# A hybrid decoder layer on one core: right operands of the Strassen products made on GpSimd during retention, a later turning back of chunks, and a fifth pair of input tiles

## The chip, the cores and the metric

The kernel runs on one core of a Trainium2 chip. The metric is the device time of one execution in microseconds; the kernel before takes 1079.97 us (median of three runs, 1079.96 to 1080.04). In the profile PE is TensorE, DVE is VectorE, ACT is ScalarE, POOL is GpSimd and SP is SyncE, whose queue issues all DMAs here.

## What is computed

One decoder layer over 1024 positions with a model width of 1024, all in float32. Cut to what matters:

```python
u = rms_norm(x, norm1_g)
z = u @ w_in                      # 3*512 columns for conv, 4*512 for retention
y_conv = cb * causal_dwconv3(cc * ch, conv_w)          # then a group norm, 8 groups
q, k = rotary(rq), rotary(rk) * 128 ** -0.5
# retention, 4 heads, chunks of 128 positions
scores = (q_c @ k_c.T) * intra_decay
o = scores @ v_c + (q_c * xi) @ state
state = chunk_decay * state + (k_c * zeta).T @ v_c
y_ret = group_rms_norm(o, ret_norm_g, 4) * silu(rg)
x = x + concat(y_conv, y_ret) @ w_out
x = x + relu(rms_norm(x) @ w_up) ** 2 @ w_down
out = rms_norm(x, final_norm_g)
```

## The kernel before, in words

Everything is held transposed: features lie on the 128 partitions, positions along the row. A matmul takes a block of weights [128 x 128] and 512 positions. To keep float32 accuracy every operand is split into a rounded high half and the remainder, its low half, and each product is three matmuls (high-high, high-low, low-high). ACT casts the high half, DVE or POOL subtracts it for the low half (`split_piece`, L166, for weights).

SBUF has one large pool, `big` (L104), of 40 buffers of [128 x 1024], called units; all large tiles come from it and a new one waits until a buffer is free. Smaller tiles are `t` (pool `tp`, L111, six buffers), `h` for retention (six) and `s` for norms (four). The eight PSUM banks are two pools of four, `pm` and `pr`.

The program is written in the order of each engine's queue. A planner in Python decides at build time where background work goes: `Engine` (L48) keeps a clock for each engine by a linear cost, `now` is PE's time, `slot()` advances it by 2.72 us for twelve matmuls. Background tasks are generators; `tick()` (L501) after each twelve or so matmuls continues those whose engine would start within `LOOK` = 3.2 us. A generator yields what it waits for: a tuple of engines of which the one that ends first is taken, a key that another task marks, or a margin after which its matmuls may be put into PE's queue. `force(key)` (L461) runs all tasks until a key is marked.

The stages up to the output projection:

1. Load x, scale it by `norm1_g`, split it (uh, ul) and make v for all heads (L350, up to about 50 us). ACT copies v out of eight banks (L363).
2. Four rotary tile pairs: q and k for head pair p = 0, then p = 1 (`rot_tiles`, L540). Each tile is `tile_in` (L518): four quarters of 24 matmuls over two banks. DVE multiplies by cosine and sine out of the banks, DVE and POOL add.
3. `retention(p)` (L577), a background task, once q and k of its head pair are there. In one step chunk c gets its scores, and the transposed keys; DVE masks the scores and ACT scales the keys. One step later the chunk's product with v and the state is made, DVE updates the state S, and ACT and DVE norm the result (`m` holds two numbers for each position, `on` the normed chunk). One step after that PE turns the chunk back (L661) and ACT copies it out.
4. The remaining sixteen column tiles of w_in, in the order `IN_TURNS` (L40) and `IN_END`. Single tiles go by `whole` (L741), pairs by `pair_in` (L821). A pair uses a Strassen-like scheme of seven products for two tiles and two halves of positions (`UP_ORDER`, L45: 1, 2, 5, 6, 3, 7, 4), each of 12 matmuls over one bank. Its left operands are sums of weight blocks, made by POOL (`Left`, L198); its results are combined by DVE adds out of banks. Its right operands are the input halves "11", "21", "22", which are uh and ul themselves, and four sums t1 to t4 for each of four k tiles j. `rights(j)` (L782) makes these: it loads two xs tiles from HBM again, scales them on ACT (1024 columns at once), makes four sums on POOL or DVE, and for each sum a high half on ACT (`put_hi`) and a low half on POOL or DVE (`put_lo`) into a unit called U. Tiles j = 0, 1 start after retention of p = 0, j = 2, 3 after that of p = 1, and odd ones after the even one before. Before the first pair's products 5, 6, 7 and 4 the operand that they read is forced (L827).
5. Convolution, gates and norms run as background tasks on the outputs of these tiles. Then the last two tiles (`IN_END`) by halves, and the output projection from about 332 us.

The weight pieces follow in the same order as the tiles through SP's queue, four buffers in `rw`; `mix` is asked for a new piece whenever one is taken.

Of the kernel before, what the change touches and what calls it, by code (L numbers as in the profile page):

```python
# [16 lines left out]
P = 128  # L17
# [19 lines left out]


IN_QK = [12, 13, 16, 17, 14, 15, 18, 19]
IN_TURNS = [0, 1, 2, 3, 20, (4, 5), (6, 7), (8, 9), (10, 11), 21]  # L40
IN_END = [22, 23]
SLOT, LOOK, PE_MARGIN, LATE = 2.72, 3.2, 1.2, 0.0
WARM = 10
# [36 lines left out]
def hybrid_layer(  # L80
# [27 lines left out]
    banks_ = ctx.enter_context(ExitStack())  # L108
    pm = banks_.enter_context(tc.tile_pool(name="pm", bufs=4, space=PSUM))
    pr = banks_.enter_context(tc.tile_pool(name="pr", bufs=4, space=PSUM))  # L110
    tp = mixer.enter_context(tc.tile_pool(name="tp", bufs=6))  # L111
    xp = mixer.enter_context(tc.tile_pool(name="xp", bufs=1))

    ctx.enter_context(tc.manual_schedule())
# [226 lines left out]

    v = [unit(s="v") for _ in range(NC_ // 2)]
    rtok = cp.tile([P, NC_], F32, name="rtok")
    ms = xp.tile([P, NC_], F32, name="ms")
    r2 = xp.tile([P, NC_], F32, name="r2")
# [12 lines left out]
                        stop=(k == KT - 1 and a is ul),  # L360
                    )
    for c in range(NC_):
        act.copy(v[c // 2][:, hs[c % 2]], vb[c])  # L363

    def token_norms():
        b = bank(pr)
# [210 lines left out]
    def retention(p, q, k):  # L577

        h0 = 2 * p
        S = pend = turn = None  # L580
        o = q
        js = [slice(j * P, (j + 1) * P) for j in range(2)]
        if p:
            yield "retention", 0
        for c in range(NC_ + 2):
            yield STEP_MARGIN
            now[0] += 1.7
            new = None
            if c < NC_:
                sl = slice(c * P, (c + 1) * P)  # L590
                bs = bank(pr)
                for j in range(2):
                    nc.tensor.matmul(bs[:, js[j]], k[j][:, sl], q[j][:, sl], start=True, stop=True)
                kz = None
                if c < NC_ - 1:
                    bt = bs[:, 2 * P :]
                    for j in range(2):
                        nc.tensor.transpose(bt[:, js[j]], k[j][:, sl], ident)
                sc = xp.tile([P, 2 * P], F32, tag="h", name=nm("h"), bufs=6)
                for j in range(2):  # L600
                    dve.scalar_tensor_tensor(
                        sc[:, js[j]], bs[:, js[j]], by_key[:, h0 + j, c : c + 1], causal,
                        ALU.mult, ALU.mult,
                    )
                if c < NC_ - 1:
                    kz = xp.tile([P, 2 * P], F32, tag="h", name=nm("h"), bufs=6)
                    for j in range(2):
                        act.activation(
                            kz[:, js[j]], bt[:, js[j]], AF.Copy, scale=by_state[:, h0 + j, c : c + 1]
                        )  # L610
                new = (c, sc, kz)
                retention_task[p].ready = clock[dve]
            done, pend = pend, new
            turned, turn = turn, None
            if done is not None:
                pc, sc, kz = done
                psl = slice(pc * P, (pc + 1) * P)
                vt = v[pc // 2]
                v0 = (pc % 2) * H + h0 * P
                vj = [vt[:, v0 + j * P : v0 + (j + 1) * P] for j in range(2)]  # L620
                bo = bank(pr)
                for j in range(2):
                    nc.tensor.matmul(bo[:, js[j]], sc[:, js[j]], vj[j], start=True, stop=(S is None))
# [20 lines left out]
                on = xp.tile([P, 2 * P], F32, tag="h", name=nm("h"), bufs=6)  # L644
# [12 lines left out]
            if turned is not None:  # L657
                pc, on = turned
                b = bank(pr)
                for j in range(2):  # L660
                    nc.tensor.transpose(b[:, js[j]], on[:, js[j]], ident)  # L661
# [89 lines left out]

        tile_in(evac)

    for p in range(2):
# [10 lines left out]
    U = {}  # L765

    def put_hi(name, j, src):
# [5 lines left out]
        hi, lo = U[name][j]  # L773
        eng.tensor_sub(lo, src, f32(hi))

    def product(n, bank_):
        name = {1: "11", 2: "21", 3: "22", 4: "t4", 5: "t1", 6: "t2", 7: "t3"}[n]
        b = bank(bank_)
        mm(parts.pop(0), [b], lambda _, k: U[name][k], True, True)
        return b  # L780

    def rights(j):  # L782

        yield "retention", j // 2
        if j % 2:
            yield "t4", j - 1
        a, b = (unit(s="xs") for _ in range(2))
        lo_, hi_ = hs
        for k, t in ((j, a), (4 + j, b)):
            nc.sync.dma_start(t, xT[k * P : (k + 1) * P, :])  # L790
        rights_task[j].ready = now[0] + 5.0
        for k, t in ((j, a), (4 + j, b)):
            yield (act,)
            act.activation(t, t, AF.Copy, scale=sm[:, G1 + k : G1 + k + 1])
        eng = yield (pool, dve)
        eng.tensor_sub(a[:, lo_], a[:, hi_], a[:, lo_])
        eng = yield (pool, dve)
        eng.tensor_sub(a[:, hi_], b[:, hi_], a[:, hi_])
        eng = yield (pool, dve)
        eng.tensor_sub(b[:, hi_], b[:, hi_], a[:, lo_])  # L800
        eng = yield (pool, dve)
        eng.tensor_sub(b[:, lo_], b[:, lo_], b[:, hi_])
        for name, src in (("t1", a[:, lo_]), ("t2", b[:, hi_]), ("t3", a[:, hi_]), ("t4", b[:, lo_])):
            yield (act,)
            put_hi(name, j, src)
            eng = yield (pool, dve)
            put_lo(name, j, src, eng)
            mark((name, j), eng)

    rights_task = []  # L810
    for j in range(4):
        rights_task.append(Task(rights(j), now[0]))
        rights_task[j].go()
    spread_norms(rows_)
    for j in range(4):
        for c, name in ((0, "11"), (1, "21"), (2, "22")):
# [707 lines left out]
```

## Time and profile before

| | |
|---|---|
| median of three runs | 1079.97 us |
| the profiled execution, its own time | 1082.14 us |
| its span (first to last instruction) | 1080.3 us |
| mean granted TensorE clock | 0.995 |
| HBM read, written | 71.40 MB, 9.44 MB |
| PE's chain share | 80% of the chain that ended last |

The span is what the trace covers; the execution's own time has what lies around it. The page gives for each engine its busy time, its share of the span and its number of instructions. In a list of groups, a row has the line, the engine and the operation, the tile written and the tiles read, the shapes and how many; behind the first bar the busy time in us and the mean of one in ns, behind the second the idle time of the engine just ahead of them and what ended it. L74 is the line of the helper that records every operation of ACT, DVE and POOL, so their groups are told apart by tiles. In an order of time a row begins with its start and its duration in us, and an idle time ahead of it stands in square brackets. In the list of waits the numbers are the total in us, how often, and the longest.

### The profile page before, as it was taken

The numbers are of one execution on the slowest core, as the hardware profiler recorded it, in microseconds if no ns is written. First come the engines' busy times: TensorE is split into PE (matmuls) and PEld (weight loads), VectorE is DVE, ScalarE is ACT, GpSimd is POOL, SyncE is SP. The second block draws the span as 40 slices with busy tenths as digits, with TensorE's granted clock in tenths as the row PEclk, the third lists the DMA queues.
The fourth block names the chain that finished last, engine by engine and source line by source line (L and its number), as shares of the span: only waits on it lengthen the run. The fifth ranks groups of instructions, "written<-read, shape, count | busy, mean of one in ns | idle before, by whom it ended". The sixth has DMA issues, their size and how long they took to land.

```text
span 1080.3 us, 14040 instructions
## 1 busy us (share of the span) xinstructions
PE 1060.6 (98%) x4936; PEld 882.7 (82%) x4936; DVE 881.2 (82%) x1255; ACT 463.3 (43%) x916; POOL 540.3 (50%) x370
## 2 busy tenths in 40 slices
PE   9999999999999999999999999999999999999996
PEld 7888888887778888788788888888888888888886
DVE  8446546799997666699999989999899899899945
ACT  8211445763335544444343443443343434334453
POOL 6233323256752132559548258267286295384543
PEclk9999999999999999999999999999999999999998
DMA  7121121212223635050121211211301211210204
GB/s 273 62 59 48 31 79 69 100 58 77 69 59 117 224 114 169 2 194 30 58 69 39 79 39 49 89 25 54 93 25 50 88 30 43 85 30 12 77 1 157
DMA packets 40311, 81.75 MB, mean 76 GB/s; under 512 B 4528, under 2 KB 6704, under 8 KB 40240
## 3 DMA queue, kind: packets, MB, share of 16 engines
q1 hardware_dynamic: 40240, 80.85, 23.2%
q8 instruction: 39, 0.64, 0.2%
q14 instruction: 32, 0.26, 0.1%
HBM read 71.40 MB, written 9.44 MB: 75 GB/s over the span
## 4 chain that ended last, share of the span: by engine, by line
PE 80%; DVE 11%; issue 3%; POOL 3%; ACT 2%; DMA 1%; POOLq 0%; DVEq 0%; SPq 0%; ACTq 0%
PE b L401 50%; PE b L1274 23%; PE b L355 4%; DVE z L74 2%; DVE wl L74 2%; POOL r L74 1%; POOL z L74 1%; DVE t L74 1%; DVE x L74 1%; DVE xs L74 1%; DVE U L74 1%; DVE q L74 1%; ACT h L74 1%; PE b L337 1%; DVE m L74 1%
## 5 line engine op out<-in xcount | busy, mean ns | idle before, releaser
L401 PE MATMUL b<-U,wh 128*128 128x512 f32 x1024 | 315.9, 390 | 2.4 <-DVE x L74 1.2
L74 ACT CAST wh<-r 128x512 fp32r<-128x512 f32 x286 | 175.9, 620 | 321.2 <-PE b L401 134.7
L74 DVE TENSOR_TENSOR wl<-r,wh 128x512 fp32r<-128x512 f32 x251 | 233.3, 932 | 90.9 <-ACT wh L74 90.0
L74 POOL TENSOR_TENSOR r<-r,r 128x512 f32<-128x512 f32 x136 | 209.8, 1545 | 116.0 <-DVE wl L74 65.6
L1274 PE MATMUL b<-V,wh 128*128 128x512 f32 x784 | 242.0, 389 | 0.7 <-POOL V L74 0.4
L401 PEld LDWEIGHTS b<-U,wh 128*128 128x128 f32 x1024 | 191.8, 188 | 43.4 <-issue 2.8
L74 DVE TENSOR_TENSOR x<-x,b 128x512 f32<-128x512 f32 (+1 forms) x320 | 197.8, 663 | 24.4 <-PE b L401 19.3
L401 PE MATMUL b<-U,wl 128*128 128x512 f32 x512 | 199.4, 389 | 0.0
L1274 PEld LDWEIGHTS b<-V,wh 128*128 128x128 f32 x784 | 147.0, 188 | 32.3 <-POOL V L74 0.8
L74 POOL TENSOR_TENSOR t<-t,t 128x512 f32<-128x512 f32 x70 | 106.3, 1523 | 97.9 <-ACT t L74 51.9
L1274 PE MATMUL b<-V,wl 128*128 128x512 f32 x392 | 152.5, 389 | 0.0
L74 POOL TENSOR_TENSOR wl<-r,wh 128x512 fp32r<-128x512 f32 x35 | 49.1, 1408 | 159.2 <-ACT wh L74 151.9
L401 PEld LDWEIGHTS b<-U,wl 128*128 128x128 f32 x512 | 96.0, 188 | 20.7 <-POOL wl L74 0.4
L401 PE MATMUL b<-uh,wh 128*128 128x512 f32 x304 | 103.3, 399 | 2.3 <-DVE z L74 2.3
L401 PE MATMUL b<-uh,wl 128*128 128x512 f32 x304 | 100.8, 392 | 1.1 <-DVE wl L74 1.1
L401 PE MATMUL b<-ul,wh 128*128 128x512 f32 x304 | 101.0, 392 | 0.0
L1274 PEld LDWEIGHTS b<-V,wl 128*128 128x128 f32 x392 | 73.6, 188 | 15.2
L74 POOL TENSOR_TENSOR V<-t,V 128x512 fp32r<-128x512 f32 x35 | 49.6, 1417 | 67.2 <-ACT V L74 67.2
L74 DVE TENSOR_TENSOR t<-t,b 128x512 f32<-128x512 f32 x112 | 75.8, 677 | 1.7 <-POOL t L74 1.2
L74 ACT ACTIVATE t<-t 128x512 f32<-128x512 f32 x64 | 40.2, 631 | 81.9 <-DVE t L74 81.3
L74 DVE TENSOR_TENSOR V<-t,V 128x512 fp32r<-128x512 f32 x63 | 70.3, 1116 | 0.0
L401 PEld LDWEIGHTS b<-uh,wl 128*128 128x128 f32 x304 | 57.3, 189 | 13.9 <-DVE wl L74 1.5
(168 smaller groups left out, 1431.0 us busy)
## 6 DMA issues: line engine op xcount, KB each, us to landing
r<-w_up_t SPq DMA_DIRECT2D x64, 256.0 KB, 2.6
r<-w_down_t SPq DMA_DIRECT2D x56, 256.0 KB, 2.7
r<-w_in_t SPq DMA_DIRECT2D x48, 256.0 KB, 2.6
xt<-xT SPq DMA_DIRECT2D x16, 256.0 KB, 5.4
xs<-xT SPq DMA_DIRECT2D x8, 512.0 KB, 4.8
r<-w_out_t SPq DMA_DIRECT2D x16, 256.0 KB, 2.7
x<-xT SPq DMA_DIRECT2D x8, 512.0 KB, 7.4
k<-x SPq DMA_DIRECT2D x6, 512.0 KB, 3.2
```

The costliest lines, as they stand in the source:

```text
L74: return f(out, *args, **kw)
L337: nc.tensor.matmul(b[:, c * P : (c + 1) * P], d, ident, start=True, stop=True)
L355: nc.tensor.matmul(vb[i], a[k][:, i * P : (i + 1) * P], b[k // 2][:, vs], start=(k == 0 and a is uh and b is vh), stop=(k == KT - 1 and a ...
L401: nc.tensor.matmul(b, a[:, k, :], rhs(n, k)[r], start=(start and i == 0), stop=(stop and i == len(ops) - 1),)
L1274: nc.tensor.matmul(b, a, r, start=(i == 0), stop=(i == len(ops) - 1))
```

## The change

Four things change together:

- **Order.** `IN_TURNS` begins with tile 20 and then 0 and 1; tiles 2 and 3 become a pair, so five pairs and four single tiles stand where four pairs and six single tiles stood.
- **Right operands.** `rights(j)` is started after q and k of the first head pair. Tile j = 0 starts after these, 1 after t4 of tile 0, 2 after q and k of the second pair, 3 after t1 of tile 2. High and low halves of j = 1 wait for retention of p = 0, those of 2 for t4 of tile 1, those of 3 for retention of p = 1. While a retention task is alive the sums and low halves go to POOL alone, afterwards to POOL or DVE. The scaling is in halves of 512 columns, and all four high halves come ahead of the low halves.
- **Turning back.** The normed chunk is turned back two steps after its product instead of one. Retention has one more step, and `h` has eight buffers.
- **v.** It is stored by head pair and half of the chunks, so that the first pair's part is free when its retention ends. Each bank is copied half by ACT and half by DVE. `t` has five buffers.

```diff
-IN_TURNS = [0, 1, 2, 3, 20, (4, 5), (6, 7), (8, 9), (10, 11), 21]
+IN_TURNS = [20, 0, 1, (2, 3), (4, 5), (6, 7), (8, 9), (10, 11), 21]
...
-    tp = mixer.enter_context(tc.tile_pool(name="tp", bufs=6))
+    tp = mixer.enter_context(tc.tile_pool(name="tp", bufs=5))
...
-    v = [unit(s="v") for _ in range(NC_ // 2)]
+    v = {(p, i): unit(s="v") for p in range(2) for i in range(2)}
...
-        act.copy(v[c // 2][:, hs[c % 2]], vb[c])
+        for p, eng in ((0, act.copy), (1, dve.tensor_copy)):
+            to = slice(c % 4 * 2 * P, (c % 4 + 1) * 2 * P)
+            eng(v[p, c // 4][:, to], vb[c][:, p * 2 * P : (p + 1) * 2 * P])
...
-        S = pend = turn = None
+        S = pend = None
+        turns = []
...
-        for c in range(NC_ + 2):
+        for c in range(NC_ + 3):
...
-                sc = xp.tile([P, 2 * P], F32, tag="h", name=nm("h"), bufs=6)
+                sc = xp.tile([P, 2 * P], F32, tag="h", name=nm("h"), bufs=8)
...
-            turned, turn = turn, None
+            turned = turns.pop(0) if turns and (len(turns) > 1 or c > NC_) else None
...
-                turn = (pc, on)
+                turns.append((pc, on))
...
             if c == NC_:
+                k = None
+                for i in range(2):
+                    del v[p, i]
                 mark(("retention", p), act)
...
+    def beside():
+
+        return (pool,) if any(t in procs for t in retention_task) else (pool, dve)
+
+    def rights(j):
+
+        yield [("qk", 0), ("t4", 0), ("qk", 1), ("t1", 2)][j]
+        a, b = (unit(s="xs") for _ in range(2))
+        lo_, hi_ = hs
+        for k, t in ((j, a), (4 + j, b)):
+            nc.sync.dma_start(t, xT[k * P : (k + 1) * P, :])
+        rights_task[j].ready = now[0] + 5.0
+        for k, t in ((j, a), (4 + j, b)):
+            yield (act,)
+            act.activation(t[:, lo_], t[:, lo_], AF.Copy, scale=sm[:, G1 + k : G1 + k + 1])
+            yield (act,)
+            act.activation(t[:, hi_], t[:, hi_], AF.Copy, scale=sm[:, G1 + k : G1 + k + 1])
+        eng = yield beside()
+        eng.tensor_sub(a[:, lo_], a[:, hi_], a[:, lo_])
...
+        if j:
+            yield [("retention", 0), ("t4", 1), ("retention", 1)][j - 1]
+        parts_ = ("t1", a[:, lo_]), ("t2", b[:, hi_]), ("t3", a[:, hi_]), ("t4", b[:, lo_])
+        for name, src in parts_:
+            yield (act,)
+            put_hi(name, j, src)
+        for name, src in parts_:
+            eng = yield beside()
+            put_lo(name, j, src, eng)
+            mark((name, j), eng)
...
+        mark(("qk", p), dve)
+        if p == 0:
+            for j in range(4):
+                rights_task.append(Task(rights(j), now[0]))
+                rights_task[j].go()
...
-    def rights(j):
-
-        yield "retention", j // 2
-        if j % 2:
-            yield "t4", j - 1
...
-            act.activation(t, t, AF.Copy, scale=sm[:, G1 + k : G1 + k + 1])
-        eng = yield (pool, dve)
...
-            put_hi(name, j, src)
-            eng = yield (pool, dve)
-            put_lo(name, j, src, eng)
-            mark((name, j), eng)
```

More of the change, by code (lines that the diff above doesn't have):

```diff
@@ L605, in retention @@
                 if c < NC_ - 1:
-                    kz = xp.tile([P, 2 * P], F32, tag="h", name=nm("h"), bufs=6)
+                    kz = xp.tile([P, 2 * P], F32, tag="h", name=nm("h"), bufs=8)
                     for j in range(2):
@@ L617, in retention @@
                 psl = slice(pc * P, (pc + 1) * P)
-                vt = v[pc // 2]
-                v0 = (pc % 2) * H + h0 * P
+                vt = v[p, pc // 4]
+                v0 = pc % 4 * 2 * P
                 vj = [vt[:, v0 + j * P : v0 + (j + 1) * P] for j in range(2)]
@@ L642, in retention @@
                     retention_task[p].ready = clock[dve]
-                on = xp.tile([P, 2 * P], F32, tag="h", name=nm("h"), bufs=6)
+                on = xp.tile([P, 2 * P], F32, tag="h", name=nm("h"), bufs=8)
                 m = xp.tile([P, 2], F32, tag="m", name=nm("m"), bufs=4)
@@ L752, in whole, with put_hi, put_lo @@
         tile_in(evac)
+    U = {}
+    def put_hi(name, j, src):
+        u = unit(F32R, "U")
+        act.copy(u[:, :H], src)
+        U.setdefault(name, [None] * 4)[j] = (u[:, :H], u[:, H:])
+    def put_lo(name, j, src, eng=dve):
+        hi, lo = U[name][j]
+        eng.tensor_sub(lo, src, f32(hi))
+    def beside():
[15 more added lines that the diff above has]
+        eng = yield beside()
+        eng.tensor_sub(a[:, hi_], b[:, hi_], a[:, hi_])
+        eng = yield beside()
+        eng.tensor_sub(b[:, hi_], b[:, hi_], a[:, lo_])
+        eng = yield beside()
+        eng.tensor_sub(b[:, lo_], b[:, lo_], b[:, hi_])
+        if j:
[5 more added lines that the diff above has]
+        for name, src in parts_:
+            eng = yield beside()
+            put_lo(name, j, src, eng)
+            mark((name, j), eng)
+    rights_task = []
     for p in range(2):
@@ L762, in hybrid_layer @@
         del q, k
-    U = {}
-    def put_hi(name, j, src):
-        u = unit(F32R, "U")
-        act.copy(u[:, :H], src)
-        U.setdefault(name, [None] * 4)[j] = (u[:, :H], u[:, H:])
-    def put_lo(name, j, src, eng=dve):
-        hi, lo = U[name][j]
-        eng.tensor_sub(lo, src, f32(hi))
+        mark(("qk", p), dve)
[3 more added lines that the diff above has]
+                rights_task[j].go()
     def product(n, bank_):
@@ L780, in product @@
         return b
-    def rights(j):
-        yield "retention", j // 2
-        if j % 2:
-            yield "t4", j - 1
[L787 to L793, printed above, removed]
-            act.activation(t, t, AF.Copy, scale=sm[:, G1 + k : G1 + k + 1])
-        eng = yield (pool, dve)
-        eng.tensor_sub(a[:, lo_], a[:, hi_], a[:, lo_])
-        eng = yield (pool, dve)
[L798 to L804, printed above, removed]
-            put_hi(name, j, src)
-            eng = yield (pool, dve)
-            put_lo(name, j, src, eng)
-            mark((name, j), eng)
[L810 to L813, printed above, removed]
     spread_norms(rows_)
```

## The prediction

> **What bounds the kernel now.** I read the page first, then PE's waits, then busy times by stage, then each engine in order of time around the waits.
>
> ```profile
> span 1080.3 us, 14040 instructions
> PE 1060.6 (98%) x4936; PEld 882.7 (82%) x4936; DVE 881.2 (82%) x1255; ACT 463.3 (43%) x916; POOL 540.3 (50%) x370
> ```
>
> PE is busy for 98% of the span, so the time is its number of matmuls plus its few waits. In this execution 1082.14 us were counted around a span of 1080.3; the median of the three runs is 1079.97. I make the sum as a difference in the span and take it from the median.
>
> All edits lie between 47 and 320 us. The waits of PE there, from 104 to 335 us:
>
> ```profile
> PE b L401 <- DVE z L74: 2.3, 1, 2.3
> PE b L661 <- ACT h L74: 1.2, 3, 0.6
> PE b L401 <- DVE wl L74: 1.1, 1, 1.1
> PE b L481 <- ACT s L74: 1.0, 1, 1.0
> PE b L482 <- DVE s L74: 0.4, 2, 0.2
> PE b L482 <- DVE r L74: 0.3, 1, 0.3
> ```
>
> That is 6.3 us in all. 1.2 of it is retention's turning back (L661); 5.1 belongs to the stretch of the pairs. Busy time there (PE, PEld, DVE, ACT, POOL, then granted clock):
>
> ```profile
> 104.00:160.00 56.00, 55.43 (x325) 48.17 (x325) 30.57 (x82) 24.52 (x97) 15.12 (x12) 1.00 0.16 53
> 160.00:209.00 49.00, 48.37 (x287) 42.27 (x286) 33.01 (x83) 28.92 (x100) 15.53 (x12) 1.00 0.21 75
> 209.00:318.00 109.00, 104.47 (x452) 83.63 (x450) 103.28 (x112) 53.53 (x91) 66.85 (x43) 1.00 0.23 75
> 318.60:322.20 3.60, 3.60 (x9) 2.88 (x10) 2.74 (x4) 1.75 (x3) 0.87 (x1) 0.55 0.00 0
> ```
>
> The reader is to see two regimes. While retention runs (the first two rows) DVE is busy 55% and 67%, POOL 27% and 32%. From 209 us on DVE is at 95%, and PE's waits there nearly all end on DVE. The last row: after the wait of 2.3 us the clock is granted at 0.55 for 3.6 us, which loses another 1.6 us (3.6 x 0.45).
>
> **Part by part: the fifth pair.** Two single tiles (2 and 3) are 2 x 4 quarters of 24 matmuls, a pair is 7 products of 12 over one bank: 7 x 12 = 84 in place of 2 x 48 = 96. Twelve fewer. Their price, from PE's order of time inside a pair, where the products follow without a gap:
>
> ```profile
> 243.72 0.39 PE L401 MATMUL b<-uh,wh 128*128 128x512 f32 x1
> 246.44 0.62 PE L401 MATMUL b<-U,wh 128*128 128x512 f32 x2
> ```
>
> From the first matmul of one product to the first of the next are 2.72 us. So -2.7 us, certain as long as PE sets the end. (A matmul's row of 0.39 us overlaps the next; the distance counts.)
>
> What the pair adds elsewhere: seven vector adds from banks, three more weight splits (seven pieces for four), four POOL sums of blocks; two ACT copies of a go. Groups from 205 to 320 us, with those for the right operands that leave this stretch:
>
> ```profile
> L74 DVE TENSOR_TENSOR z<-z,b 128x512 f32<-128x512 f32 x25 | 17.0, 680 | 0.5
> L74 DVE TENSOR_TENSOR wl<-r,wh 128x512 fp32r<-128x512 f32 x17 | 19.7, 1157 | 1.7 <-ACT wh L74 1.6
> L74 DVE TENSOR_TENSOR U<-xs,U 128x512 fp32r<-128x512 f32 x10 | 11.1, 1130 | 0.2
> L74 DVE TENSOR_TENSOR xs<-xs,xs 128x512 f32<-128x512 f32 x4 | 4.6, 1146 | 0.3
> L74 DVE TENSOR_TENSOR xs<-xs 128x512 f32<-128x512 f32 x4 | 3.8, 960 | 0.1
> L74 POOL TENSOR_TENSOR r<-r,r 128x512 f32<-128x512 f32 x16 | 24.5, 1535 | 4.0 <-DMA r<-w_in_t 2.0 <-DVE wl L74 1.3
> ```
>
> Added to DVE: 7 x 0.68 + 3 x 1.16 = 8.2 us; to POOL 4 x 1.54 = 6.1. Removed from DVE: 11.1 + 4.6 + 3.8 = 19.5 us, less up to 4 x 1.13 = 4.5 for the low halves of the fourth k tile, which may still go to either engine. Net relief about 6.8 us. But the stretch gets 2.7 us shorter, and tile 1's work on a (before, partly ahead of 205) now falls behind it, an estimate of 2.5 us from two bank products and an R2 product. So DVE has 103.3 - 6.8 + 2.5 = 99 us of work in some 106: 93% in place of 95%. I therefore take the 5.1 us of waits and the 1.6 us of slow clock as unchanged, ends at all of it gone (-6.7) and, as one more pair brings its share of them, at +1.7 (6.7 over four pairs).
>
> **The right operands earlier.** 32 element-wise instructions (16 sums, 16 low halves), before mostly on DVE after retention's middle; 24 of them, k tiles 0 to 2, can now only go to POOL while retention is alive. Both engines' times for one (shortest, median, longest):
>
> ```profile
> L74 DVE TENSOR_TENSOR U<-xs,U x13: 679/693/1789, 177.1 to 243.2; 128x512 fp32r<-128x512 f32 x13
> L74 POOL TENSOR_TENSOR U<-xs,U x3: 1287/1299/1728, 177.7 to 235.2; 128x512 fp32r<-128x512 f32 x3
> L401 PE MATMUL b<-U,wh x128: 387/389/402, 238.3 to 315.5; 128*128 128x512 f32 x128
> ```
>
> 24 x 1.30 = 31 us (at 1.73, 41) come to POOL's 15.1 + 15.5 from 104 to 209 us: 62 to 72 of 105. It fits. Against this speaks the Trainium skill, GPSIMD Engine Reference, section 4.1 (Engine selection): ordinary two-input arithmetic belongs on VectorE, about 2x faster; the trace agrees (1.30 to 0.69), and by that rule the sum would lose 24 x 0.6 = 15 us if these instructions lay on the path.
>
> Are they in time? The last row says that U is first read at 238.3 us. In the new order only tiles 20, 0, 1, twelve quarters, stand ahead of the first pair instead of twenty, so it starts about eight quarters of 2.7 earlier. PE's order of time at retention's end:
>
> ```profile
> 205.64 0.38 PE L623 MATMUL b<-v,h 128*128 128x128 f32 x2
> 209.79 0.52 PE L661 MATMUL b<-ident,h 128*128 128x128 f32 x2
> ```
>
> Retention's last product is at 206 us, the twelfth quarter ends at 209.8, and the first pair's third product (the first with t1) comes two products later, at 215.2. Only the fourth k tile waits for that last product; then it needs a cast and a low half, about 2 us, for t1, and at most 4 x 1.73 = 7 us for all four, the last of which is read at about 226. So zero, hidden by two products on uh and ul; if POOL is behind by more than some 7 us, the excess comes straight onto PE.
>
> The xs loads go through SP's queue ahead of weight fetches; the weights are taken three pieces ahead, some 16 us, and a load waits only for a buffer to come free. Zero, up to +2. The scaling in two halves of 512 instead of one of 1024 adds only instruction starts on ACT, half idle in these rows.
>
> **The turn two steps later.** PE waited 1.2 us in three places for the normed chunk. The longest:
>
> ```profile
> 194.75 0.97 DVE L74 TENSOR_TENSOR m<-m 128x2 f32<-128x2 f32 x1 [0.27 <-ACT m L74]
> 195.76 1.19 DVE L74 SCALAR_TENSOR_TENSOR m<-m,m 128x2 f32<-128x2 f32 x1
> 193.17 1.29 POOL L74 TENSOR_TENSOR wl<-r,wh 128x512 fp32r<-128x512 f32 x1 [9.21 <-ACT wh L74]
> 194.43 1.27 POOL L74 TENSOR_TENSOR a<-a,ssq 128x512 f32<-128x512 f32 x1
> 195.67 1.25 POOL L74 TENSOR_TENSOR xs<-xs 128x512 f32<-128x512 f32 x1
> 197.86 0.44 PE L661 MATMUL b<-ident,h 128*128 128x128 f32 x2 [0.63 <-ACT h L74]
> ```
>
> A [128 x 2] instruction that takes 0.16 us alone (row below) takes 0.97 and 1.19 while POOL runs without a break. With a step more, about 5 us, this is covered: -1.2 us. No matmul is added, only the last transposes move; the two more h buffers keep a chunk alive and are paid by one t buffer. Evacuation needs four t at once and a norm one each, so five do: zero.
>
> **v in halves.** The eight copies of v are shared by ACT and DVE, behind PE's product and ahead of nothing before retention at 104: zero.
>
> Sum: -2.7 - 1.2 = -3.9, or 1079.97 - 3.9 = 1076.1; ends -3.9 - 6.7 = -10.6 (1069.4) and -3.9 + 1.7 + 2 = -0.2 (1079.8) without the rivals. I say 1076.0.
>
> **The rivals.** *The pairs' waits go* (0.20). With no backlog of right operands, DVE reaches the last pair's adds in time: the 2.3 us wait, its 1.6 us of slow clock, and half of the other 2.8 vanish: 1076.1 - 5.3, about 1071. For it: 18 DVE instructions leave; against:
>
> ```profile
> 247.84 2.46 DVE L74 SCALAR_TENSOR_TENSOR cv<-a,sm,cv 128x511 f32<-128x511 f32 x2 [0.85 <-ACT cv L74]
> ```
>
> DVE stood idle for 0.85 us at 247, so that backlog was over before the waits of the pairs. The Trainium skill, TensorE: Matmul & The Clock Gate, section "What's actually happening", gives an idle window of about 3.4 us before the clock is halved; here 2.3 us were enough.
>
> *The vector engine eats it* (0.16). The fifth pair's 8.2 us on DVE and 6.1 on POOL come in a stretch at 95%; half of DVE's share, 4 us, turns into new waits: 1080, no change.
>
> *Slower: POOL holds up retention* (0.14). DVE works in order: the next chunk's masking stands behind this chunk's m instructions. One step on DVE with POOL still:
>
> ```profile
> 117.94 0.61 DVE L74 SCALAR_TENSOR_TENSOR h<-b,bk,causal 128x128 f32<-128x128 f32 x2 [1.73 <-PE b L598]
> 121.34 0.16 DVE L74 SCALAR_TENSOR_TENSOR m<-m 128x2 f32<-128x2 f32 x1
> 122.93 0.61 DVE L74 SCALAR_TENSOR_TENSOR h<-b,bk,causal 128x128 f32<-128x128 f32 x2 [1.43 <-PE b L598]
> ```
>
> 3.6 us of work in a step of 5.0. Two m instructions lengthened as above add 1.84: 5.4, already over. It decides from 1.4 us of added time a step on. If every one of the sixteen steps loses the 0.4 to 0.5, PE waits 7 us: 1076.1 + 7 = 1083. Against: 24 POOL instructions over sixteen steps are 2 us in 5, so most m instructions meet none, and one step of slack lies between masking and product. The Trainium skill, GPSIMD Engine Reference, section 1 (Specifications), names SBUF interfaces shared with VectorE and contention for instructions with two SBUF inputs; the lengthened rows agree.
>
> *The turn gains nothing* (0.05). The buffers of U come free no earlier, so the operands are made at the same place, the waits at L661 stay, and only the matmuls go: 1077.2.
>
> **How the numbers follow.** Forecast 0.45, rivals 0.20, 0.16, 0.14, 0.05. A measurement of this kernel can tell about 0.2%, 2.2 us. Faster: 0.45 + 0.20 + 0.05 = 0.70; same 0.16; slower 0.14. The range from 1071.0 to 1081.0 takes in the vanished waits as far as priced and the eaten gain, and leaves out the slower rival and the far end of the second, together under 0.2.
>
> **What would show it.** Right: 4924 PE matmuls; no wait at L661; U first written near 105 us and first read near 215; POOL some 60% busy from 104 to 209; DVE at 90% or more from 209 to 318 with about 5 us of waits. Wrong: PE waiting at L593, L623 or L631 (slower rival), a wait of PE for U, or waits in the pairs far from 5 us either way.

## The result and the profile after

The kernel after takes 1096.75 us (median of four runs, 1093.4 to 1097.08); the kernel before took 1080.01 us beside it. The ratio is 1.0139, with a 95% interval of 1.0125 to 1.0153: slower by 1.4%, where 1076 was predicted. The profiled execution took 1096.65 us around a span of 1094.9, 14.6 us more than the span before.

The first lines of its page:

```profile
span 1094.9 us, 14067 instructions
PE 1062.7 (97%) x4924; PEld 883.6 (81%) x4924; DVE 879.8 (80%) x1252; ACT 466.3 (43%) x928; POOL 572.9 (52%) x395
```

The twelve matmuls are gone (4936 before). The waits of PE from 104 to 350 us; in this kernel L626 is retention's product with v (L623 before), L664 the turning back (L661), L403 the products of the tiles (L401), L483 and L484 sums for norms:

```profile
PE b L664 <- ACT h L74: 9.4, 6, 2.5
PE b L626 <- DVE h L74: 3.0, 2, 2.6
PE b L403 <- DVE z L74: 2.3, 1, 2.3
PE b L626 <- ACT h L74: 2.3, 2, 1.4
PE b L483 <- ACT s L74: 1.0, 1, 1.0
PE b L484 <- DVE s L74: 0.4, 2, 0.2
PE b L484 <- DVE r L74: 0.3, 1, 0.3
PE b L403 <- DVE wl L74: 0.2, 1, 0.2
```

Retention waits 9.4 + 3.0 + 2.3 = 14.7 us in ten places; before it was 1.2 in three. The other rows sum to 4.2 (before 5.1). No row shows a wait for U. Busy time by stage, with the columns of the table in the prediction:

```profile
104.00:160.00 56.00, 48.88 (x269) 42.01 (x269) 34.20 (x76) 24.23 (x86) 24.50 (x18) 0.97 0.14 48
160.00:209.00 49.00, 43.78 (x264) 38.03 (x263) 26.01 (x66) 31.74 (x99) 23.42 (x17) 1.00 0.20 65
209.00:318.00 109.00, 104.84 (x462) 84.42 (x460) 92.57 (x110) 50.59 (x108) 72.10 (x49) 0.98 0.18 58
318.00:350.00 32.00, 29.49 (x122) 23.91 (x123) 27.59 (x36) 13.61 (x22) 10.08 (x8) 0.95 0.47 149
```

In the first two rows, which hold most of retention, none of DVE, ACT and POOL is full: DVE is busy for 34.2 of 56 us and 26.0 of 49, ACT for 24.2 and 31.7, POOL for 24.5 and 23.4. PE is the one that lost, 7.1 and 5.2 us. So no engine lacks time over the stage as a whole; what is late there is late at its place in the order, as the two steps below show.

The span's 14.6 us: retention's waits give +13.5 (14.7 - 1.2), the other waits -0.9, the matmuls -2.7; the slow clock +3.9 (after 56 x 0.03 + 109 x 0.02 + 32 x 0.05 = 5.5, before 32 x 0.05 = 1.6; with clocks in hundredths this is good to about 1 us); and by the starts of the matmuls each wait costs PE some 0.2 us more than the list has, +1.4 for seven more waits. That is 15.2, within the clock's rounding. 13.6 us of it are there at the mixer's last sum for a norm (331.59 us before, 345.22 after); what follows takes nearly the same time in both.

**How one wait comes about.** Retention's step is a chain that goes through two engines: ACT norms chunk c, DVE makes `m` from it, ACT scales it, DVE masks the scores of the next chunk, ACT scales its keys. Two steps in order of time, each with the PE row that had waited last; the second shows only the rows that bear on the wait. The first:

```profile
117.15 1.66 ACT L74 CAST U<-xs 128x512 fp32r<-128x512 f32 x3
117.84 4.18 POOL L74 TENSOR_TENSOR U<-xs,U 128x512 fp32r<-128x512 f32 x3 [4.97 <-ACT U L74]
118.70 0.62 ACT L74 CAST wh<-r 128x512 fp32r<-128x512 f32 x1
119.41 1.48 DVE L74 TENSOR_TENSOR wl<-r,wh 128x512 fp32r<-128x512 f32 x1 [2.81 <-ACT wh L74]
120.81 0.60 DVE L74 SCALAR_TENSOR_TENSOR h<-b,bk,causal 128x128 f32<-128x128 f32 x2
121.30 0.77 PE L626 MATMUL b<-v,h 128*128 128x128 f32 x2 [2.58 <-DVE h L74]
```

Read it from below. The product had waited 2.58 us for the masked scores; the masking stood in DVE's queue behind a weight's low half; that had waited 2.81 us for the high half; and this cast stood in ACT's queue behind three casts for U, 1.66 us. The low half itself took 1.48 us beside the busy POOL, against 0.69 us for each of the three that DVE made in before. POOL was at its own three low halves, so the planner had given the weight's low half to DVE. In the prediction's rows of before the masking at 117.94 waits for PE alone. The second step:

```profile
140.74 0.63 ACT L74 ACTIVATE h<-b,m 128x128 f32<-128x128 f32 x2 [0.62 <-DVE m L74]
141.56 2.58 ACT L74 ACTIVATE xs<-xs,sm 128x512 f32<-128x512 f32 x4
145.72 0.34 DVE L74 SCALAR_TENSOR_TENSOR m<-m,bq 128x2 f32<-128x2 f32 x1 [4.12 <-ACT h L74]
146.01 1.27 POOL L74 TENSOR_TENSOR xs<-xs 128x512 f32<-128x512 f32 x1
146.34 0.95 DVE L74 TENSOR_TENSOR m<-m 128x2 f32<-128x2 f32 x1 [0.27 <-ACT m L74]
147.35 2.61 POOL L74 TENSOR_TENSOR xs<-xs,xs 128x512 f32<-128x512 f32 x2
147.52 1.11 DVE L74 SCALAR_TENSOR_TENSOR m<-m 128x2 f32<-128x2 f32 x1
148.67 0.63 ACT L74 ACTIVATE h<-b,m 128x128 f32<-128x128 f32 x2 [2.36 <-DVE m L74]
149.35 0.44 PE L664 MATMUL b<-ident,h 128*128 128x128 f32 x2 [2.52 <-ACT h L74]
```

Here four scalings, 2.58 us in one run on ACT, stand ahead of retention's own work there, and DVE idles for 4.12 us ahead of `m`. Then two `m` instructions take 0.95 and 1.11 us in place of 0.16 while POOL goes from one instruction to the next; a third between them, at 147.32, takes its 0.16. The run on ACT is what the prediction costed at nothing, the lengthened `m` is its slower rival. Together they are over 4 us in a step of 5.

The turn that waited belongs to chunk 3, whose own norm had ended at 141.37 (the first row). The norm that ends at 149.30, just ahead of it, is that of chunk 4. So the turn did not wait for its data; why it waited is taken up with the experiments.

POOL's share of the weights' low halves moved too. From 104 to 205 us POOL made ten of them before and DVE three; after:

```profile
L74 DVE TENSOR_TENSOR wl<-r,wh x8: 691/1158/1712, 104.2 to 197.9; 128x512 fp32r<-128x512 f32 x8
L74 POOL TENSOR_TENSOR wl<-r,wh x3: 1274/1288/1847, 144.8 to 166.7; 128x512 fp32r<-128x512 f32 x3
```

The new order brought one thing more. With tile 20 ahead, its Silu runs between retention's roots, and each change loads a table. Two of ACT's rows, and the PE row that waited:

```profile
195.34 1.28 ACT L74 ACT_TABLE_LOAD   x1
196.64 0.63 ACT L74 ACTIVATE z<-z 128x512 f32<-128x512 f32 x1
199.85 0.49 PE L626 MATMUL b<-v,h 128*128 128x128 f32 x2 [1.44 <-ACT h L74]
```

Behind the Silu stand a weight's cast on ACT, its low half and the masking on DVE and the keys on ACT, and these end the wait. Three more loads follow at 200.33, 215.72 and 218.17; before, the first of this stretch stands at 234.93, behind retention.

### The profile page after: what moved, and what is told of

The parts are those of the page before. It is cut to its first block, busy times and chain, and to the rows that moved or that the text cites. A ratio compares the mean times of both kernels' runs of the same rounds, so it can differ in the third digit from the quotient of the medians.

```text
span 1094.9 us, 14067 instructions
## 1 busy us (share of the span) xinstructions
PE 1062.7 (97%) x4924; PEld 883.6 (81%) x4924; DVE 879.8 (80%) x1252; ACT 466.3 (43%) x928; POOL 572.9 (52%) x395
## 4 chain that ended last, share of the span: by engine, by line
PE 72%; DVE 12%; ACT 5%; issue 4%; POOL 4%; DMA 1%; POOLq 0%; DVEq 0%; SPq 0%; ACTq 0%
PE b L403 45%; PE b L1290 22%; PE b L355 4%; DVE z L74 2%; DVE wl L74 2%; DVE m L74 2%; ACT h L74 2%; POOL r L74 1%; DVE x L74 1%; DVE t L74 1%; POOL z L74 1%; DVE cv L74 1%; DMA x<-k 1%; ACT wh L74 1%; POOL x L74 1%
## 5 line engine op out<-in xcount | busy, mean ns | idle before, releaser
L403 PE MATMUL b<-U,wh 128*128 128x512 f32 x1056 | 325.7, 390 | 2.9 <-DVE x L74 1.1
L74 DVE TENSOR_TENSOR wl<-r,wh 128x512 fp32r<-128x512 f32 x256 | 239.9, 940 | 84.1 <-ACT wh L74 83.1
L74 POOL TENSOR_TENSOR r<-r,r 128x512 f32<-128x512 f32 x140 | 214.4, 1534 | 119.9 <-DVE wl L74 66.7
L403 PEld LDWEIGHTS b<-U,wh 128*128 128x128 f32 x1056 | 197.7, 188 | 45.2 <-issue 1.9
L403 PE MATMUL b<-U,wl 128*128 128x512 f32 x528 | 205.6, 389 | 0.0
L403 PEld LDWEIGHTS b<-U,wl 128*128 128x128 f32 x528 | 99.1, 188 | 21.0 <-DVE wl L74 0.3
L403 PE MATMUL b<-uh,wh 128*128 128x512 f32 x284 | 98.4, 401 | 2.3 <-DVE z L74 2.3
L403 PE MATMUL b<-uh,wl 128*128 128x512 f32 x284 | 96.4, 395 | 0.2 <-DVE wl L74 0.2
L403 PE MATMUL b<-ul,wh 128*128 128x512 f32 x284 | 96.6, 395 | 0.0
L1290 PEld LDWEIGHTS b<-V,wl 128*128 128x128 f32 x392 | 73.5, 188 | 15.2
L403 PEld LDWEIGHTS b<-uh,wl 128*128 128x128 f32 x284 | 54.3, 191 | 12.5 <-DVE wl L74 0.7
```

The lines of the kernel that those rows point to most:

```text
L74: return f(out, *args, **kw)
L403: nc.tensor.matmul(b, a[:, k, :], rhs(n, k)[r], start=(start and i == 0), stop=(stop and i == len(ops) - 1),)
L1290: nc.tensor.matmul(b, a, r, start=(i == 0), stop=(i == len(ops) - 1))
```

## The experiments

Three theories had to be told apart. *Chain*: the 24 ACT and 24 POOL instructions of the early right operands delay retention's steps, in the way just read. *Bank*: the turn two steps later waits for a PSUM bank that the last step's product holds, so the waits come from the new place of the turn. *Order*: tile 20 with its tables and the early first pair make the delay. The kernel before ran beside every one; ratios are to that.

**The turn alone.** On the kernel before: two_steps takes from the change only the turn two steps later, with eight h buffers and five t. two_steps_first also puts the turn ahead of the step's product in PE's order; after_turn_first does that in the kernel after.

```diff
+            if turned is not None:
+                ...
             if done is not None:
                 pc, sc, kz = done
...
-            if turned is not None:
-                ...
```

> The kernel before with the later turning back alone (two steps, eight h, five t). Bank theory: the four banks of pr go round, and the third bank taken in a step, that of the turn, is the one that held the product of the step before; so the transposes still wait for that product's norm, the waits at the transposes stay near 1.2 us and the time stays within 0.5 us of 1080. Rival (the prediction's term): the waits are gone and the time is 1.2 us less.

> The same, with the transposes and copies of the turn put ahead of the product in each step, so that the turn takes the bank of the scores of the step before and the product that of the turn before. Bank theory: the waits at the transposes are gone, 1.2 us less than the kernel before. Rival: the norm itself is late, the wait shows at the product or at the scores instead, and the time stays at 1080.

> The changed kernel with only this reordering. Its waits at the transposes are 9.4 us. Bank theory: nearly all of the 9.4 us go, and with them some of the slow clock after them: 1086 to 1088. Rival (POOL makes the norm and the masking late on DVE): the same waits move to the product and its sums, less than 3 us are gained: above 1093.

two_steps: 1079.57 us, ratio 0.9986 (0.9976 to 0.9995); one wait of 0.3 us is left at the turn. two_steps_first: 1076.81 us, 0.9962 (0.9948 to 0.9977), and no wait of PE in retention. Repeated as two_steps_first_again with eleven runs it had 1078.65 us, 0.9982 (0.9974 to 0.9991): a gain, of 2 us rather than 4.

> The kernel before with the later turn placed ahead of the product, for comparison on the same chip: 1076 to 1077.5 as before.

after_turn_first: 1095.82 us, 1.0137 (1.0122 to 1.0152), the same as after. Its waits in retention:

```profile
PE b L622 <- ACT h L74: 9.8, 6, 2.5
PE b L636 <- ACT h L74: 4.3, 2, 3.2
```

One of them in order of time:

```profile
154.81 0.59 DVE L74 SCALAR_TENSOR_TENSOR h<-b,bk,causal 128x128 f32<-128x128 f32 x2
155.50 0.63 ACT L74 ACTIVATE h<-b,bz 128x128 f32<-128x128 f32 x2 [3.73 <-DVE h L74]
156.18 0.44 PE L622 MATMUL b<-ident,h 128*128 128x128 f32 x2 [2.54 <-ACT h L74]
```

The turn (L622) waits for the keys of the step before instead of its norm, and these for DVE's masking. PE meets the same delay at another place, and the time is the same. So the bank theory falls as the cause of the loss: the place of the turn doesn't set what after loses.

What that theory says of the wait itself the traces bear out. Each of the six waits at L664 in after ends with the norm of the chunk behind the one that is turned, as in the second step above; by the order of the four banks that chunk's product holds the bank which the turn takes. The one wait left in two_steps ends in the same way (chunk 4's norm ends at 138.44, chunk 3's turn starts at 138.50). A step more therefore frees the turn of its own chunk's norm, not of the next one's. Whether freeing it of the bank as well is worth time these runs can't tell: two_steps and two_steps_first_again lie at 0.9986 and 0.9982.

**One mending each, on the kernel after.** after_silu_late holds tile 20's Silu until retention is over. after_dve gives the early sums and low halves to DVE. after_wl_pool sends the weights' low halves to POOL while retention runs. after_paced sets a k tile back by a slot of 2.72 us behind each of its early ACT instructions; in its trace they still go in twos (two scalings in 1.36 us at 145.23, two casts in 1.18 at 158.60), no longer in threes and fours. after_four_pairs keeps the order of before.

```diff
         # after_silu_late
+        if not h:
+            yield "retention", 1
         yield (act,)
         act.activation(g[:, sl], g[:, sl], AF.Silu)
...
         # after_dve
-        return (pool,) if any(t in procs for t in retention_task) else (pool, dve)
+        return (dve,) if any(t in procs for t in retention_task) else (pool, dve)
...
         # after_wl_pool
+        if any(t and t in procs for t in retention_task):
+            eng = pool
-        if "mixer" not in got and clock[pool] + 1.2 < clock[dve] + 0.6:
+        elif "mixer" not in got and clock[pool] + 1.2 < clock[dve] + 0.6:
...
         # after_paced, behind each early scaling and cast
+        if any(t in procs for t in retention_task):
+            rights_task[j].ready = now[0] + SLOT
...
         # after_four_pairs
-IN_TURNS = [20, 0, 1, (2, 3), (4, 5), (6, 7), (8, 9), (10, 11), 21]
+IN_TURNS = [0, 1, 2, 3, 20, (4, 5), (6, 7), (8, 9), (10, 11), 21]
```

> The changed kernel with the Silu of tile 20 held until the second retention is done. Theory of the tables: ACT loads another table for Silu and then again for the root in the norm, twice within retention, 4 loads of 1.28 us; the two waits behind the first of them (1.4 and 1.7 us) go and the time falls by about 3 to 4 us, to 1093. Rival (ACT has the time for it): the waits stay and the time with them, 1096 to 1097.

> The changed kernel with the early right operands' sums and low halves on VectorE instead of GpSimd while retention is alive. Theory of contention (GpSimd's 1.3 us instructions stretch the norm's small DVE instructions from 0.16 to about 1.1 us): the stretched instructions become rare, the waits in retention fall from 14.7 us to under 8 and the time to 1086 to 1090. Rival (ACT's runs of four scalings or three casts, and what queues behind them, make retention late): waits within 2 us of 14.7, the time stays at 1094 to 1098.

> The changed kernel with the low halves of weights on GpSimd while retention is alive; before, GpSimd made ten of thirteen of them there, in the changed kernel VectorE makes most, and the masking queues behind one that waits for ACT's cast. Theory of the displaced split: the wait of 2.6 us at 121 goes and two or three smaller ones with it, 3 to 5 us less, 1092. Rivals: contention grows (no gain, 1096 or more); ACT runs (the same as now).

> The changed kernel with at most one of a k tile's ACT instructions (four scalings, four casts) in a slot of twelve matmuls while retention is alive, so that they do not stand in a row ahead of retention's own. Theory of ACT runs: the waits in retention fall to under 8 us, the time to 1086 to 1090, if the fourth k tile is not late for the first pair. Rival (contention on DVE): waits and time hardly change, 1094 to 1098.

> The changed kernel with the order of tiles of the kernel before (tiles 0, 1, 2, 3, 20, four pairs). If the early right operands alone make the loss, retention's waits stay above 9 us (no table loads for Silu in it) and the time is above 1090: the fifth pair is worth its 2.7 us. If the early first pair or the Silu in retention makes it, the time falls to 1084 or less.

| | us | ratio (95%) | waits in retention, us |
|---|---|---|---|
| after | 1096.75 | 1.0139 (1.0125 to 1.0153) | 14.7 |
| after_silu_late | 1094.99 | 1.0127 (1.0110 to 1.0144) | 10.5 |
| after_dve | 1090.01 | 1.0094 (1.0072 to 1.0117) | 10.5 |
| after_wl_pool | 1090.04 | 1.0101 (1.0081 to 1.0120) | 11.8 |
| after_paced | 1092.15 | 1.0110 (1.0092 to 1.0128) | 10.5 |
| after_four_pairs | 1089.87 | 1.0093 (1.0074 to 1.0111) | 10.4 |

Four of the five are faster than after by 0.3 to 0.5%; after_silu_late isn't measurably, since waits for norms (L483) grew from 1.0 to 3.6 us while those in retention shrank by four. None brings the kernel near before. So no single one of these is the cause, and the order theory holds for a part only: 0.46% of 1080, some 5 us, go with the order and the fifth pair, both of which after_four_pairs takes back. In after_dve only 3 of the 64 `m` instructions take over 0.5 us, against 12 in after, and POOL again makes ten of the weights' low halves; 10.5 us of waits are left all the same.

**Leaving one engine's part out.** In no_vec the 24 sums and low halves of the first three k tiles aren't made, in no_act the 24 scalings and casts; the planner's clocks are charged as if they were.

```diff
         # no_vec, at each of the four sums, and in the same way at the low halves
-        eng.tensor_sub(a[:, lo_], a[:, hi_], a[:, lo_])
+        if j < 3:
+            skipped(eng)
+        else:
+            eng.tensor_sub(a[:, lo_], a[:, hi_], a[:, lo_])
...
         # no_act, at each scaling, and in the same way at the casts
-        act.activation(t[:, lo_], t[:, lo_], AF.Copy, scale=sm[:, G1 + k : G1 + k + 1])
+        if j < 3:
+            skipped(act)
+        else:
+            act.activation(t[:, lo_], t[:, lo_], AF.Copy, scale=sm[:, G1 + k : G1 + k + 1])
```

> The changed kernel with the sums and low halves of the first three k tiles left out (24 GpSimd instructions; the high half stands in for the low one), the planner's clocks advanced as if they ran, so that all else keeps its place in the queues. Theory of contention and late vector work: retention's waits fall from 14.7 us to under 5, the time to 1084 to 1087. Rival (ACT's runs): waits above 10, time above 1091.

> The changed kernel with ACT's scalings and casts of the first three k tiles left out (24 instructions; uh and ul stand in for the halves, the 24 vector instructions still run in place), the planner's clocks advanced as before. Theory of ACT's runs: retention's waits fall from 14.7 to under 5 us and the time to 1084 to 1087. Rival (contention on DVE): waits above 10, time above 1091. If both this and its counterpart lose about half, the delays add up along one chain that passes both engines.

no_vec: 1086.94 us, 1.0056 (1.0038 to 1.0075). Its waits in retention:

```profile
PE b L664 <- ACT h L74: 5.7, 5, 2.4
PE b L626 <- ACT h L74: 1.9, 1, 1.9
```

no_act: 1088.01 us, 1.0067 (1.0052 to 1.0083). Its waits there:

```profile
PE b L664 <- ACT h L74: 5.9, 6, 2.3
PE b L626 <- ACT h L74: 1.8, 2, 0.9
PE b L626 <- DVE h L74: 0.5, 1, 0.5
```

Without the vector part the kernel is 0.83% faster than after (9 us), without the ACT part 0.72% (8 us); 7.6 and 8.2 us of waits remain. Both halves hold retention up, each about as much as the other, so neither the vector part on POOL nor ACT's queue explains it alone. Together the two gains are 17 us and exceed the 15 that were lost, which fits a wait that needs the delay of one engine and that of the next. A kernel with both left out was not run. Of the three theories the chain is the one that these runs bear out.

**All mendings together.** comb joins the edits of after_dve, after_wl_pool, after_silu_late and after_turn_first; comb_paced adds that of after_paced.

> The changed kernel with four mendings at once: early sums and low halves on VectorE, low halves of weights on GpSimd while retention is alive, Silu after retention, the turn ahead of the product. If each takes its own part of the chain (6, 6, 2 and 1 us alone), 1082 to 1084; if they overlap in the same waits, 1086 to 1090.

> The same with ACT's part of the right operands paced, one in a slot. If the runs on ACT are what is left, retention's waits fall under 3 us, but the fourth k tile may be late for the first pair (4.5 us when this was done alone): 1078 to 1084. Rival: what is left is the sheer work on DVE and ACT in a step, no change against the other combination.

comb: 1084.6 us, 1.0036 (1.0023 to 1.0049), 5.6 us of waits in retention. comb_paced: 1079.13 us, 0.9982 (0.9973 to 0.9992). Its waits from 104 to 350 us (two more, of 0.3 and 0.2, are for norms):

```profile
PE b L406 <- DVE U L74: 3.7, 1, 3.7
PE b L406 <- DVE z L74: 2.3, 1, 2.3
```

None is in retention. The same early operands as in after cost retention 14.7 us or nothing, according to the engine that makes them, to where in the queues they stand and to what stands there beside them. Which of the five edits are needed for that was not tried; pacing on top of the other four took out the last 5.6 us. What is left is 3.7 us for a low half of the fourth k tile, which the pacing had made late.

**The fifth pair by itself.** comb2 takes the fourth k tile out of the pacing and makes each of its low halves right behind its high half; comb2_four is the same with the order and the four pairs of before. On comb_paced:

```diff
-        if any(t in procs for t in retention_task):
+        if j < 3 and any(t in procs for t in retention_task):
             rights_task[j].ready = now[0] + SLOT
...
             put_hi(name, j, src)
             pace(j)
-        for name, src in parts_:
+            if j == 3:
+                eng = yield (pool, dve)
+                put_lo(name, j, src, eng)
+                mark((name, j), eng)
+        for name, src in parts_ if j < 3 else ():
```

> The paced combination with the fourth k tile unpaced and each low half right behind its high half, so that t1 does not wait for all four casts. The wait of 3.7 us for U goes, and some slow clock after it: 1073 to 1075, below the kernel with the turn alone (1076.8). Rival: the low halves only move, U is still late, 1078 to 1079.

> The same with the order of tiles of the kernel before (four pairs). If the fifth pair is worth its twelve matmuls where nothing waits for it: 2.7 us above the five-pair version, 1076 to 1078. Rival (the pair's vector work eats it): within 1 us of it.

comb2: 1079.76 us, 0.9997 (0.9989 to 1.0006). comb2_four: 1074.09 us (1073.74 to 1075.5), 0.9949 (0.9936 to 0.9963): faster than the kernel before by 6 us and the fastest of the study. Neither came out as expected: in comb2 the wait for U went, but the time stayed above both ranges; comb2_four came out below its range, and the difference between the two has the other sign. The waits of comb2 from 104 to 350 us (two more of 0.3 each):

```profile
PE b L486 <- ACT s L74: 3.0, 2, 2.0
PE b L406 <- DVE z L74: 2.3, 1, 2.3
PE b L406 <- POOL wl L74: 1.0, 1, 1.0
PE b L487 <- DVE s L74: 0.7, 3, 0.2
```

And of comb2_four:

```profile
PE b L406 <- DVE z L74: 2.3, 1, 2.3
PE b L487 <- DVE r L74: 0.3, 1, 0.3
```

In both retention has no wait, so the two differ by the fifth pair and the order that came with it: 5.7 us slower with it. The stretch of the pairs in comb2, up to 260 us and from there:

```profile
209.00:260.00 51.00, 47.71 (x210) 38.60 (x209) 46.33 (x51) 24.75 (x45) 33.04 (x22) 1.00 0.24 78
260.00:318.00 58.00, 53.72 (x228) 42.08 (x227) 55.04 (x59) 22.32 (x39) 35.77 (x24) 1.00 0.22 69
```

And in comb2_four:

```profile
209.00:260.00 51.00, 51.00 (x228) 42.19 (x227) 42.81 (x46) 22.40 (x40) 29.11 (x19) 1.00 0.21 72
260.00:318.00 58.00, 55.39 (x243) 45.05 (x242) 53.45 (x59) 23.21 (x39) 36.11 (x24) 1.00 0.22 65
```

DVE has 46.3 + 55.0 = 101.4 us of work in 109 with five pairs, 96.3 with four, and in the first row 91% against 84%. PE idles 7.6 us in the first table and 2.6 in the second. The list of waits has 5.0 us more for comb2; the starts of its matmuls, taken against the usual distance of 0.227 us, have 7.3 more, since each wait also costs about 0.3 us that the list doesn't count, 0.2 up to the matmul that waited and 0.1 at the next one. Less the 2.7 of the matmuls that is 4.6; the last turn of retention, at 210.21 and 209.79, adds 0.4; the mixer's last sum (L487) stands at 328.01 and 322.84, 5.2 apart.

The longest wait that comb2 has and comb2_four has not, 2.0 us at 227.57 for a norm, comes from DVE's backlog. DVE works without a break from 211.50 to 226.21, and ACT's square for that norm had to wait for it:

```profile
226.24 0.63 ACT L74 ACTIVATE t<-z 128x512 f32<-128x512 f32 x1 [5.88 <-DVE z L74]
```

Another 1.0 us is for a weight's low half on POOL, where the mending had sent it while retention was alive. So DVE as the cause is shown for the longest wait and argued for the rest, and the new place of tile 20 was not tried apart from the pair.

## Why the prediction was wrong

**The step that failed is "It fits".** The prediction added 31 us to POOL's 30.6, saw 62 of 105, and took the early operands as free. Busy shares say whether work finds time on an engine; they don't say what stands behind it in that engine's order. In retention a step of 5 us is a single chain through ACT and DVE, with little room; 48 instructions set among its links, in runs of 1.7, 2.6 and 4.2 us, gave 14.7 us of waits, 13.5 more than before: the cost that the sum had at zero. Even POOL's share was missed: 24.5 + 23.4 = 47.9 of 105 us, 46% and not 60%. Of the 14 us between, some 8.5 are weights' low halves, which the planner moved from a busy POOL to DVE, straight into the chain; 3.8 are three instructions for right operands (2.5 us of sums, 1.3 of a low half) that the 30.6 of before already held, so that the working counted them twice.

**"Only instruction starts on ACT, half idle"** failed in the same way. The scalings were counted, but not that the casts and scalings of one k tile go off in a row. no_act puts this part at 8 us.

**The slower rival** named the right engine and the right stretch at a chance of 0.14, and its lengthened `m` instructions are there (0.95 and 1.11 us at 146). Most are not lengthened, as the argument against the rival had it: the median `m` is still 0.16 us. But 12 of the 64 take over 0.5 us (2 in before), and what they all take beyond 0.16 us each adds up to 11.3 us (2.5 in before). Of the waits, 5.3 us stand at L626, the L623 that this rival named; 9.4 stand at the turn. Its mechanism is one of the links, and its 7 us were half of the waits that came.

**The fifth pair: -2.7 us, "certain as long as PE sets the end".** The twelve matmuls did go. (The quarters of 24 that the working and the text ahead of it speak of are twelve matmuls each: two k tiles, three products, two banks. A tile is 48, so 84 against 96 stands.) PE did not set the end: with seven adds and three weight splits more DVE is busy for 93% of the stretch and not 88%, and comb2 against comb2_four shows +5.7 us instead. Rival two, the vector engine eats it, comes nearest, as far as the waits of comb2 show; it was priced at 4 us of new waits, and the time lost is about 8 (5.7 + 2.7).

**The turn: -1.2 us** was right in size by itself: two_steps has 0.9986, some 1.5 us, and the wait fell from 1.2 to 0.3. The reason given was not: a step more doesn't cover the norm, because the turn still waits for the next chunk's norm at its bank. Why two of the three waits went in two_steps all the same is open. In after 9.4 of the 14.7 us of waits stand at just this turn, where the prediction looked for none. **v in halves: zero** was right; PE is busy for all 57 us from 47 to 104 in both.

**Are the operands in time?** No wait for U in after, as said, but U is first read by PE at 232.6 us and not at 215, since retention had delayed everything ahead of it. Where retention has no wait and the fourth k tile isn't paced, in comb2, the first read is at 213.2 us and there is no wait for U either, so zero was right. Where the fourth k tile is paced, waits of 4.5 us (after_paced) and 3.7 (comb_paced) for U came.

**The Silu** was not in the prediction at all: the change of order was read for what it does to the matmuls, not for which ACT functions come to stand between which. after_silu_late shows about 4 us less of waits in retention without it, and the waits for norms of the pairs took 2.6 back.

**The waits of the pairs**, taken as unchanged at 5.1, were 4.2, and the wait of 2.3 us behind the last pair's products (DVE z; in before U is read for the last time at 315.71, and the wait ends at 318.60) is in every kernel of the study, so the first rival, that it would go, falls.

## What to carry to other kernels

Before work is moved beside a latency-bound loop, follow one step of the loop through the in-order queues of all the engines that it crosses, and cost each added instruction as a delay of the link behind it: an engine that is half idle can still be late at every step. Then spread the added work over the gaps, here in ones and twos, and keep what has been displaced (here the weights' low halves) and what an order brings along (here the Silu's table) in the count. Fewer matmuls are worth little where the engine that combines their results has no room; here twelve fewer came with 5.7 us more.

## What the runs showed of the hardware

- **The granted clock after a wait.** After waits of nearly the same length the clock was halved or was not. In the kernel after, 3.5 us from three waits of 2.58, 2.52 and 2.34 us on:

```profile
121.30:124.80 3.50, 3.50 (x16) 3.46 (x17) 2.15 (x11) 2.44 (x11) 0.72 (x1) 0.57 0.22 75
149.30:152.80 3.50, 3.45 (x16) 2.92 (x17) 2.63 (x3) 0.84 (x3) 1.96 (x2) 1.00 0.01 2
215.40:218.90 3.50, 3.47 (x12) 2.75 (x13) 0.70 (x3) 3.45 (x9) 3.08 (x3) 0.66 0.01 2
```

  The same 2.3 us wait near 318 us halved the clock in the profile of before and not in that of two_steps_first. In the first row that costs 3.5 x 0.43 = 1.5 us, and after's runs lie apart accordingly: 1093.4 us at a mean clock of 0.995, 1096.65 at 0.992. What decides it was not tried. The Trainium skill, TensorE: Matmul & The Clock Gate, section "What's actually happening", has a free-running window of about 3.4 us, which would make it a matter of where the wait falls; that waits this short are enough is not in that section.
- **Loading a table** took 1.28 us in each of four places, with the next activation 0.02 us behind it. The Trainium skill, ScalarE: Activation LUTs, section "What ACT_TABLE_LOAD costs", gives the same 1283 ns and adds a drain of 1380 ns; these rows show no such time, neither ahead of the load (the cast before ends at 195.32, the load starts at 195.34) nor behind it.
- **A wait costs more than its row.** Against the distance of 0.227 us from matmul to matmul, the stretch of the pairs in comb2 lost 10.5 us where its nine waits have 7.6 in the list, about 0.3 us more each.
